# Reordering copies ahead of an attention: written with gaps instead of read with gaps, second value weight split among them, in a fixed order

## The chip, the cores and the metric

The kernel runs on one core of one Trainium2 chip. The core has five engines with a queue of instructions each: TensorE (PE) multiplies matrices, with a weight load (PEld) ahead of each product, VectorE (DVE), ScalarE (ACT) and GpSimd (POOL) work on elements, and SyncE (SP) starts most transfers. An engine takes its instructions in the order in which they stand in its queue, and waits at one whose inputs aren't ready. The metric is the time of one execution on the device in microseconds (us); lower is better.

## The reference

Two transformer layers work on 512 tokens of 1024 features in 32-bit floats. Layer 0 has a gated linear recurrence (HGRN2) as its mixer, layer 1 a dilated attention; each has a SwiGLU feed-forward part behind it. What matters here is the hand-over from the feed-forward part of layer 0 to the attention of layer 1:

```python
h = h + (1.0 + g2) * rms_norm(y, norm_g[layer, 3])          # end of layer 0
u = rms_norm(h, norm_g[layer, 0]) * (1.0 + sc1) + sh1       # start of layer 1
proj = (u @ w_in).reshape(B, S, N_GROUPS, 3, ATT_HEADS, ATT_HEAD_DIM)
for gi, (window, dilation) in enumerate(((128, 1), (512, 4), (2048, 16))):
    q = apply_partial_rope(proj[:, :, gi, 0], cos, sin) * scale
    k = apply_partial_rope(proj[:, :, gi, 1], cos, sin)
    v = proj[:, :, gi, 2]
    o_g, lse_g = dilated_group_attention(q, k, v, window, dilation)
```

A group with dilation 4 attends within tokens that are four apart. For it the kernel keeps a second copy of u whose tokens stand in another order: the 128 tokens l = 0..127 with the same remainder r (token 4l + r) side by side, r after r.

## The kernel before, in words

Every product of two 32-bit numbers is made of three: each operand is split into a high part (the number cast to the type float32r, "hi", "uh") and a low part (what the cast left over, "lo", "ul"), and TensorE adds high x high, high x low and low x high (the helper `three`, L597 to L601). The cast is made by ScalarE, the subtraction by VectorE or GpSimd.

u is kept transposed, as `uh` and `ul`: eight tiles (kt = 0..7) of 128 features by 512 tokens. A weight tile of 512 input features by 512 output features (128 partitions x 2048 numbers, four kt) arrives in a `raw` buffer and is split into `hi` and `lo`; there are two raw buffers and three places for split pairs. The class `Stream` hands them out in the order of a list. `Stream.process_to` (L113, L114) splits a weight in one piece of 2048; `Stream.pieces` (L133, L134) gives the functions that split it in two halves of 1024, so that the caller says where each stands. `Stream.fill` starts the next load as soon as a raw buffer is free; SyncE issues it and waits for the instruction that frees the buffer.

The stage around the change, in order:

- The end of the feed-forward part (`ffn`, manual schedule). For each of four token tiles t the class `Turn` does: squares of the two halves of y on ScalarE (`sq_y`, L635), their product with a gate on VectorE (`gated`, L644), a reciprocal root on VectorE and GpSimd (`r_y`, L648 and L650), the update of h on VectorE with the squares of the new h on ScalarE (`upds`, L660 and L635), a second root (`r_h`), the normalised tile `xn` on VectorE (L674), its transposition on TensorE (`flip`, L680), scale and shift into `u` (L690 on ScalarE, L692 on VectorE), and the split into `uh` (L695, ScalarE) and `ul` (L699, GpSimd). "Manual schedule" means that the instructions of each engine stand in its queue in the order of the code.
- The value projection of attention group 0 (`v_prod`): for each token tile 24 products (8 kt x 3) into one bank of accumulators, `ps_mm`, and one copy into `V[0]` by ScalarE (L1696). Tiles 0 and 1 fill the time in which the last token tiles are normalised; tiles 2 and 3 follow. The two weights of this group are `hi_5909` (kt 0 to 3) and `hi_6077` (kt 4 to 7) in the listings below.
- In the same block, a first weight of group 1 (`hi_6304`, kt 0 to 3) is split in two halves, and four transfers on ScalarE's queue put h aside (`h_away`).
- The copies in the other token order: for each kt one on ScalarE (from `uh` into `apart[0]`, L1721) and one on VectorE (from `ul` into `apart[1]`, L1722). They read every fourth token, so with gaps of 16 bytes, and write 512 numbers in line.
- The value projection of group 1 (`tok_proj`, four tiles of 24 products, evicted at L1704 into `V[1]`), with the second weight of the group (`hi_6402`, kt 4 to 7) split in one piece.
- Sums of the copies over pairs of tiles for a seven-product scheme (`token_sums`, L892 to L896 on VectorE, then cut into new contents of uh and ul, L900 and L901), and then the attention itself, which begins with products of `apart` and the weight `hi_6411`. Its order comes from a planner (`Plan`).

What stands behind the first of these stages, the copies, `tok_proj` and `token_sums`, is not in a manual schedule: there a scheduler that simulates a timeline sets the order in each queue.

Of the kernel before, what the change touches and what calls it, by code (L numbers as in the profile page):

```python
# [11 lines left out]
F32 = mybir.dt.float32  # L12
# [5 lines left out]
P = 128  # L18
S = 512
D = 1024  # L20
KT = D // P
NT = S // P
# [15 lines left out]
SEEN = lambda t: t.rearrange("p (x n a) -> p x a n", a=2, n=P)  # L38
# [277 lines left out]
def block_kernel(tc, x, c, positions, ada_w, ada_b, norm_g, hgrn_w_in, lower, hgrn_norm_g, hgrn_w_out,  # L316
# [8 lines left out]
    with ExitStack() as ctx:  # L325
# [712 lines left out]
        def ffn(l, first, close, nxt, side):  # L1038
            turns.close()
            close()  # L1040
            with ExitStack() as fx:
# [104 lines left out]
                with tc.manual_schedule(engines=ORDERED):  # L1146
# [17 lines left out]
                    for hi_f, lo_f in st.pieces(2, True):  # L1164
                        hi_f()
                        lo_f()
                    st.fill()
                    mm(2, (2, 3))
                    y_steps(2)
                    n.upds(2)  # L1170
                    n.flip(1, [bank("mm"), bank("b")])
# [11 lines left out]
                    vw = [st.take(0), st.take(0)]  # L1183
                    v_prod(vw, 0, range(8))
# [8 lines left out]
                    v_prod(vw, 1, range(8))  # L1193
# [11 lines left out]
                    v_prod(vw, 2, range(8))  # L1205
                    v_prod(vw, 3, range(8))
# [294 lines left out]
        def tok_proj(done):  # L1501

            ws = [st.take(), st.take(1)]
            for t in range(NT):
                ps = bank("mm")
                tok = slice(t * P, (t + 1) * P)
                for kt in range(KT):
                    whi, wlo = ws[kt // 4]
                    w = slice((kt % 4) * 512, (kt % 4 + 1) * 512)
                    three(ps, uh[:, kt, tok], ul[:, kt, tok], whi[:, w], wlo[:, w], kt == 0, kt == KT - 1)  # L1510
                done(t, ps)

# [120 lines left out]
        for p in range(4):  # L1633
            tiles = []
            whi, wlo = st.take()
# [40 lines left out]
        def open_attention():  # L1676
# [8 lines left out]
            banks = {}  # L1685

            def v_prod(ws, t, kts):
                if t not in banks:
                    banks[t] = bank("mm")
                tok = slice(t * P, (t + 1) * P)  # L1690
                for kt in kts:
                    w = slice((kt % 4) * 512, (kt % 4 + 1) * 512)
                    three(banks[t], uh[:, kt, tok], ul[:, kt, tok], ws[kt // 4][0][:, w], ws[kt // 4][1][:, w],
                          kt == 0, kt == KT - 1)
                if kts[-1] == KT - 1:
                    act.copy(PLACED(V[0][:, t]), SEEN(banks[t]))  # L1696
            return v_prod
# [3 lines left out]

        def to_away(t, ps):

            act.copy(PLACED(V[1][:, t]), SEEN(ps))  # L1704
            if t == NT - 1:
                act.dma_start(v_away, V[1])
# [673 lines left out]
```

## Time and profile before

| | |
|---|---|
| median of three runs | 1464.53 us (1464.22 to 1465.02) |
| the profiled execution | 1461.9 us |
| its span, which the profile covers | 1460.2 us |
| mean granted TensorE clock over the span | 0.998 |
| TensorE busy | 1422.7 us, 97% |
| VectorE, ScalarE, GpSimd busy | 1119.6, 825.6 and 196.8 us |
| moved by DMA | 201.10 MB, mean 138 GB/s |

A row of a timeline gives the start of an instruction in us from the start of the span, its duration in us, the engine, the line in the kernel, the operation, what it writes and reads, its shape, and in brackets how long its engine stood idle before it and what ended that wait. Several like instructions in a row are merged (x8), and the duration is then that of all. Matmuls are pipelined: one starts before the one before has ended, so the time between starts is what one costs. A row of the waits says who waited for whom: in total, how often, and the longest. The granted clock is 1.00 at full speed. A few records of matmuls can be missing.

### The profile page before, as it was taken

Reading aid. Unit: us, or ns where it says so; the run is one execution under the profiler, and the core shown is the slowest. Engines: PE = TensorE matmul, PEld = TensorE weight load, DVE = VectorE, ACT = ScalarE, POOL = GpSimd, SP = SyncE. Lnnn points to the kernel's source line nnn. Section 1 sums busy time; section 2 is a strip of 40 time slices with the busy share of each in tenths; the row PEclk is TensorE's granted clock in tenths of the full one; section 3 lists DMA queues with packets and bytes.
Section 4 is the critical chain, followed back from the end, with each engine's and each line's share of the span. In section 5 each row is a group of like instructions: output and inputs, shape, how many; then the busy total and the mean of one; then the engine's idle time right before and its main releaser. Section 6 shows DMA issues by size and latency. Waiting matters only on the chain. (4 is left out here: it accounts for less than half of the span.)

```text
span 1460.2 us, 25343 instructions
## 1 busy us (share of the span) xinstructions
PE 1422.7 (97%) x9903; PEld 1307.8 (90%) x9903; DVE 1119.6 (77%) x1800; ACT 825.6 (57%) x1484; POOL 196.8 (13%) x173
## 2 busy tenths in 40 slices
PE   8999999999999999999999999999999999999998
PEld 6777888889999998887989999998998999999887
DVE  4588589488888889778797977888776978887644
ACT  4433442474555553376748878667895645555332
POOL 1012102030111112240000110001012111110100
PEclk9999999999999999999999999999999999999999
DMA  9666554213344368424244443254353244334541
GB/s 310 195 191 200 173 174 145 87 62 93 106 116 116 117 219 295 156 83 148 91 126 132 120 124 95 72 171 131 95 176 114 87 116 115 112 105 157 178 145 58
DMA packets 212872, 201.10 MB, mean 138 GB/s; under 512 B 8920, under 2 KB 170640, under 8 KB 212496
## 3 DMA queue, kind: packets, MB, share of 16 engines
q1 hardware_dynamic: 209776, 192.71, 42.5%
q10 hardware_dynamic: 1952, 6.65, 1.3%
q8 instruction: 78, 1.28, 0.4%
q0 software_dynamic: 1024, 0.12, 0.2%
q14 instruction: 42, 0.34, 0.1%
HBM read 192.30 MB, written 5.30 MB: 135 GB/s over the span
## 5 line engine op out<-in xcount | busy, mean ns | idle before, releaser
L1843 PE MATMUL ps_mm<-apart,hiq 128*128 128x256 f32 (+1 forms) x608 | 137.5, 320 | 3.9 <-ACT xs L1957 3.2
L114 DVE TENSOR_TENSOR lo<-raw,hi 128x2048 fp32r<-128x2048 f32 x41 | 99.6, 2432 | 45.0 <-ACT hi L113 44.9
L113 ACT CAST hi<-raw 128x2048 fp32r<-128x2048 f32 x41 | 78.1, 1906 | 98.4 <-DMA raw<-in_hgrn_w_in_dram 46.7
L599 PE MATMUL ps_mm<-uh,hi 128*128 128x512 f32 (+1 forms) x368 | 130.4, 354 | 0.0
L600 PE MATMUL ps_mm<-ul,hi 128*128 128x512 f32 (+1 forms) x368 | 128.1, 348 | 1.6 <-DVE ul L699 1.6
L601 PE MATMUL ps_mm<-uh,lo 128*128 128x512 f32 (+1 forms) x368 | 128.1, 348 | 0.0
L1843 PEld LDWEIGHTS ps_mm<-apart,hiq 128*128 128x128 f32 x608 | 99.9, 191 | 10.2 <-ACT xs L1957 3.8
L971 DVE TENSOR_TENSOR loq<-raw,hiq 128x1024 fp32r<-128x1024 f32 x72 | 85.0, 1221 | 20.1 <-ACT hiq L967 20.1
L980 PE MATMUL ps_mm<-th,hiq 128*128 128x256 f32 x360 | 99.1, 275 | 0.0
L980 PE MATMUL ps_mm<-tl,hiq 128*128 128x256 f32 x360 | 99.0, 275 | 0.0
L980 PE MATMUL ps_mm<-th,loq 128*128 128x256 f32 x360 | 99.0, 275 | 0.0
L1843 PE MATMUL ps_mm<-apart,loq 128*128 128x256 f32 (+1 forms) x304 | 95.4, 314 | 0.6 <-DVE loq L1979 0.6
L951 POOL TENSOR_TENSOR raw<-raw 128x512 f32<-128x512 f32 x36 | 47.8, 1327 | 320.1 <-DVE spare L947 165.0
L967 ACT CAST hiq<-raw 128x1024 fp32r<-128x1024 f32 x72 | 72.1, 1047 | 21.4 <-DVE raw L955 16.8
L599 PEld LDWEIGHTS ps_mm<-uh,hi 128*128 128x128 f32 x368 | 69.9, 190 | 12.4 <-issue 5.3
L599 PE MATMUL ps_mm<-hi,oh 128*128 128x512 f32 x208 | 79.0, 381 | 0.0
L600 PE MATMUL ps_mm<-lo,oh 128*128 128x512 f32 x208 | 78.9, 380 | 0.0
L600 PEld LDWEIGHTS ps_mm<-ul,hi 128*128 128x128 f32 x368 | 69.9, 190 | 9.3 <-DVE ul L699 2.0
L1083 ACT CAST oh<-mid 128x512 fp32r<-128x512 f32 x44 | 37.3, 871 | 70.7 <-PE ps_b L600 62.1
L601 PEld LDWEIGHTS ps_mm<-uh,lo 128*128 128x128 f32 x368 | 69.9, 190 | 6.8
L1843 PE MATMUL ps_mm<-uh,hiq 128*128 128x256 f32 x256 | 71.2, 278 | 0.2 <-ACT ps_mm L1932 0.2
L1843 PE MATMUL ps_mm<-uh,loq 128*128 128x256 f32 x256 | 70.5, 275 | 0.0
(478 smaller groups left out, 4774.8 us busy)
## 6 DMA issues: line engine op xcount, KB each, us to landing
raw<-in_ada_w_dram SPq DMA_DIRECT2D x40, 1024.0 KB, 5.8
raw<-in_ffn_w_in_dram SPq DMA_DIRECT2D x144, 256.0 KB, 4.0
raw<-in_ffn_w_out_dram SPq DMA_DIRECT2D x22, 1024.0 KB, 5.7
raw<-in_attn_w_in_dram SPq DMA_DIRECT2D x64, 256.0 KB, 4.3
raw<-in_hgrn_w_in_dram SPq DMA_DIRECT2D x12, 1024.0 KB, 5.5
raw<-in_attn_w_in_dram SPq DMA_DIRECT2D x12, 1024.0 KB, 5.1
raw<-in_ffn_w_in_dram SPq DMA_DIRECT2D x8, 1024.0 KB, 5.1
raw<-in_attn_w_in_dram SPq DMA_DIRECT2D x16, 512.0 KB, 5.2
```

Of the source, the lines that this page charges most:

```text
L113: self.nc.scalar.copy(hi, t)
L114: self.nc.vector.tensor_sub(lo, t, hi.bitcast(F32))
L599: pe.matmul(ps, ah, bh, start=start, stop=False, skip_group_check=part)
L600: pe.matmul(ps, ah, bl, start=False, stop=False, skip_group_check=part)
L601: pe.matmul(ps, al, bh, start=False, stop=stop, skip_group_check=part)
L951: pool.tensor_add(r[:, 2], r[:, 2], r[:, 0])
L967: act.copy(hi, src)
L971: dve.tensor_sub(lo, src, hi.bitcast(F32))
L980: pe.matmul(LAID(ps), w[x][:, a], TAKE(us[kt][y]), start=begin and kt + m == 0, stop=kt == 3 and m == 2, skip_group_check=True)
L1083: act.copy(PLACED(oh), SEEN(mid(f)))
L1843: pe.matmul(LAID(dst()), x, TAKE(y), start=begin and i == 0, stop=i == len(todo) - 1, skip_group_check=True)
```

## The change

Three things are edited. In the last part of the feed-forward block, the second half of the low split of `hi_6077` and the start of the next load (`st.fill`) move from ahead of token tile 2's end to behind its update of h. The copies into the other token order read 512 tokens in line and write with gaps: the pattern `p l r` of the destination goes to remainder 0, 1, 2, 3 in turn, 128 numbers (512 bytes) apart, and then to the next l. And the copies, the last two tiles of group 0's values, all of group 1's values and the splits of two weights, now in halves, come into one manual schedule: three copies, tile 2, two copies, half of tile 3, the split of group 1's second weight, the other half, three copies, the first tile of group 1, the split of the attention's first weight, the other tiles. `tok_proj` is gone; `v_prod` serves both groups. The diff:

```diff
--- before.py
+++ after.py
@@ -1161,13 +1161,15 @@
                     n.xn(1)
                     n.parts_of(0, 1)
                     mm(3, (0, 1))
-                    for hi_f, lo_f in st.pieces(2, True):
-                        hi_f()
-                        lo_f()
-                    st.fill()
+                    (hi_a, lo_a), (hi_b, lo_b) = st.pieces(2, True)
+                    hi_a()
+                    lo_a()
+                    hi_b()
                     mm(2, (2, 3))
                     y_steps(2)
                     n.upds(2)
+                    lo_b()
+                    st.fill()
                     n.flip(1, [bank("mm"), bank("b")])
                     n.u_of(1, 0)
                     n.u_of(1, 1)
@@ -1180,8 +1182,7 @@
                     st.beside(None)
                     fx.close()
                     v_prod = nxt[1]()
-                    vw = [st.take(0), st.take(0)]
-                    v_prod(vw, 0, range(8))
+                    v_prod(0, range(8))
                     n.upds(3)
                     n.flip(2, [bank("mm"), bank("a")])
                     n.r_h(3)
@@ -1190,7 +1191,7 @@
                     n.parts_of(2, 0)
                     n.parts_of(2, 1)
                     n.xn(3)
-                    v_prod(vw, 1, range(8))
+                    v_prod(1, range(8))
                     n.flip(3, [bank("mm"), bank("b")])
                     n.u_of(3, 0)
                     n.u_of(3, 1)
@@ -1202,8 +1203,6 @@
                     st.fill()
                     for t in range(NT):
                         act.dma_start(h_away[t], h[:, t])
-                    v_prod(vw, 2, range(8))
-                    v_prod(vw, 3, range(8))
                 turns.close()
 
 
@@ -1498,18 +1497,6 @@
         head = sc.tile([P, S], F32, name="head")
         pool.memset(head, 0.0)
 
-        def tok_proj(done):
-
-            ws = [st.take(), st.take(1)]
-            for t in range(NT):
-                ps = bank("mm")
-                tok = slice(t * P, (t + 1) * P)
-                for kt in range(KT):
-                    whi, wlo = ws[kt // 4]
-                    w = slice((kt % 4) * 512, (kt % 4 + 1) * 512)
-                    three(ps, uh[:, kt, tok], ul[:, kt, tok], whi[:, w], wlo[:, w], kt == 0, kt == KT - 1)
-                done(t, ps)
-
         C16 = lambda a: a.rearrange("p (c t) -> p c t", t=32)
         B44 = lambda a: a.rearrange("p (b c t) -> p b c t", b=4, c=4)
 
@@ -1682,28 +1669,24 @@
             hx.enter_context(cx)
             vp = cx.enter_context(tc.tile_pool(name="a_v", bufs=1))
             V.extend(vp.tile([P, NT, 512], F32, name=f"V{g}") for g in range(3))
-            banks = {}
-
-            def v_prod(ws, t, kts):
-                if t not in banks:
-                    banks[t] = bank("mm")
-                tok = slice(t * P, (t + 1) * P)
-                for kt in kts:
-                    w = slice((kt % 4) * 512, (kt % 4 + 1) * 512)
-                    three(banks[t], uh[:, kt, tok], ul[:, kt, tok], ws[kt // 4][0][:, w], ws[kt // 4][1][:, w],
-                          kt == 0, kt == KT - 1)
-                if kts[-1] == KT - 1:
-                    act.copy(PLACED(V[0][:, t]), SEEN(banks[t]))
-            return v_prod
+            v_tiles.extend(st.take(0) for _ in range(2))
+            return lambda t, kts: v_prod(0, t, kts)
+
+        v_tiles, v_banks = [], {}
+
+        def v_prod(g, t, kts):
+            if (g, t) not in v_banks:
+                v_banks[g, t] = bank("mm")
+            b, tok = v_banks[g, t], slice(t * P, (t + 1) * P)
+            for kt in kts:
+                whi, wlo = v_tiles[2 * g + kt // 4]
+                w = slice((kt % 4) * 512, (kt % 4 + 1) * 512)
+                three(b, uh[:, kt, tok], ul[:, kt, tok], whi[:, w], wlo[:, w], kt == 0, kt == KT - 1)
+            if kts[-1] == KT - 1:
+                act.copy(PLACED(V[g][:, t]), SEEN(b))
 
         ffn(0, first, h0.close, ((1, 0), open_attention), "right")
         v_away = dpool.tile([P, NT, 512], F32, name="v_away")
-
-        def to_away(t, ps):
-
-            act.copy(PLACED(V[1][:, t]), SEEN(ps))
-            if t == NT - 1:
-                act.dma_start(v_away, V[1])
 
         PNs, PR_h = [h[:, k].rearrange("p (t n) -> p t n", t=4) for k in range(2)], h[:, 2].rearrange("p (t n) -> p t n", t=4)
         flip_no = [0, 0]
@@ -1717,10 +1700,31 @@
         up = upx.enter_context(tc.tile_pool(name="a_u", bufs=1))
         up.tile([P, 64], F32, name="pad")
         apart = [up.tile([P, KT, S], F32R, name=f"apart{k}") for k in range(2)]
-        for kt in range(KT):
-            act.copy(V4(apart[0][:, kt]), L4(uh[:, kt]).bitcast(F32))
-            dve.tensor_copy(V4(apart[1][:, kt]), L4(ul[:, kt]).bitcast(F32))
-        tok_proj(to_away)
+        def apart_of(*kts):
+            for kt in kts:
+                for k, (eng, u) in enumerate(((act.copy, uh), (dve.tensor_copy, ul))):
+                    eng(R4(apart[k][:, kt]), u[:, kt].rearrange("p (l r) -> p l r", r=4).bitcast(F32))
+
+        def split_next():
+            for hi_f, lo_f in st.pieces(2, True):
+                hi_f()
+                lo_f()
+            st.fill()
+
+        with tc.manual_schedule(engines=ORDERED):
+            apart_of(0, 1, 2)
+            v_prod(0, 2, range(8))
+            apart_of(3, 4)
+            v_prod(0, 3, range(4))
+            split_next()
+            v_prod(0, 3, range(4, 8))
+            apart_of(5, 6, 7)
+            v_tiles.extend(st.take(0) for _ in range(2))
+            v_prod(1, 0, range(8))
+            split_next()
+            for t in range(1, NT):
+                v_prod(1, t, range(8))
+            act.dma_start(v_away, V[1])
         th, tl = (t.rearrange("p (a b) n -> p a (b n)", a=4).rearrange("p a (b n) -> p a b n", b=4) for t in (uh, ul))
 
         token_sums(th, tl, h.rearrange("p t (a n) -> p (t a) n", a=2), *apart)()
```

On ScalarE, from the end of the feed-forward block to the first of the new casts of uh (L900), before:

```order
L133 CAST hi_6304<-raw_5913 128x1024 x2
L1204 DMA h_away<-h 128x1024 x4
L1721 CAST apart_6384<-uh 128x512 x8
L1696 COPY V_6188<-ps_mm_6317 128x512
L113 CAST hi_6402<-raw_6083 128x2048
L1696 COPY V_6188<-ps_mm_6343 128x512
L113 CAST hi_6411<-raw_6310 128x2048
L900 CAST uh<-h 128x1024
```

and now:

```order
L133 CAST hi_6304<-raw_5913 128x1024 x2
L1205 DMA h_away<-h 128x1024 x4
L1706 CAST apart_6332<-uh 128x128x4 x3
L1686 COPY V_6188<-ps_mm_6342 128x512
L1706 CAST apart_6332<-uh 128x128x4 x2
L133 CAST hi_6385<-raw_6115 128x1024 x2
L1686 COPY V_6188<-ps_mm_6372 128x512
L1706 CAST apart_6332<-uh 128x128x4 x3
L1686 COPY V_6189<-ps_mm_6415 128x512
L133 CAST hi_6441<-raw_6310 128x1024 x2
```

The eight copies are in three lots; ahead of the split of the second weight of group 1 (`hi_6402` before, `hi_6385` now) stand five of them and one eviction, where there were eight and one. That split is in two halves.

On VectorE, from the split of group 1's first weight (`lo_6305`) on, before:

```order
L134 TENSOR_TENSOR lo_6305<-raw_5913,hi_6304 128x1024 x2
L1722 CAST apart_6385<-ul 128x512 x8
L892 TENSOR_TENSOR h<-apart_6384,apart_6385 128x1024 x4
L893 TENSOR_TENSOR h<-h 128x1024
L114 TENSOR_TENSOR lo_6403<-raw_6083,hi_6402 128x2048
L114 TENSOR_TENSOR lo_6412<-raw_6310,hi_6411 128x2048
L894 TENSOR_TENSOR h<-h 128x1024
L895 SCALAR_TENSOR_TENSOR h<-h 128x1024
L896 SCALAR_TENSOR_TENSOR h<-h 128x1024
```

and now:

```order
L134 TENSOR_TENSOR lo_6305<-raw_5913,hi_6304 128x1024 x2
L1706 CAST apart_6333<-ul 128x128x4 x5
L892 TENSOR_TENSOR h<-apart_6332,apart_6333 128x1024 x2
L134 TENSOR_TENSOR lo_6386<-raw_6115,hi_6385 128x1024
L893 TENSOR_TENSOR h<-h 128x1024
L134 TENSOR_TENSOR lo_6386<-raw_6115,hi_6385 128x1024
L1706 CAST apart_6333<-ul 128x128x4 x3
L892 TENSOR_TENSOR h<-apart_6332,apart_6333 128x1024 x2
L894 TENSOR_TENSOR h<-h 128x1024
L134 TENSOR_TENSOR lo_6442<-raw_6310,hi_6441 128x1024
L895 SCALAR_TENSOR_TENSOR h<-h 128x1024
L134 TENSOR_TENSOR lo_6442<-raw_6310,hi_6441 128x1024
```

Ahead of the first low half of the second weight stand five copies and two of the four sums, where there were eight copies, the four sums and L893. Between its two halves stands L893. The low half of the attention's first weight (`lo_6412`, now `lo_6442`) stands between the last sums.

On VectorE within the feed-forward block, around the end of token tile 2 (`yg_6102` before, `yg_6099` now), before:

```order
L134 TENSOR_TENSOR lo_6078<-raw_5842,hi_6077 128x1024 x2
L644 TENSOR_TENSOR yg_6102<-ps_mm_5189,gate_5393 128x512
L648 TENSOR_SCALAR rv_6104<-ss_6097 128x1
L644 TENSOR_TENSOR yg_6108<-ps_a_5193,gate_5393 128x512
L660 SCALAR_TENSOR_TENSOR h<-yg_6102,rr_6106,h 128x512
L660 SCALAR_TENSOR_TENSOR h<-yg_6108,rr_6106,h 128x512
L692 TENSOR_SCALAR u_6132<-ps_b_6118,cols 128x128 x4
```

and now:

```order
L134 TENSOR_TENSOR lo_6078<-raw_5842,hi_6077 128x1024
L644 TENSOR_TENSOR yg_6099<-ps_mm_5189,gate_5393 128x512
L648 TENSOR_SCALAR rv_6101<-ss_6094 128x1
L644 TENSOR_TENSOR yg_6105<-ps_a_5193,gate_5393 128x512
L660 SCALAR_TENSOR_TENSOR h<-yg_6099,rr_6103,h 128x512
L660 SCALAR_TENSOR_TENSOR h<-yg_6105,rr_6103,h 128x512
L134 TENSOR_TENSOR lo_6078<-raw_5842,hi_6077 128x1024
L692 TENSOR_SCALAR u_6132<-ps_b_6118,cols 128x128 x4
```

One of the two halves of `lo_6078` has moved from ahead of tile 2's gated products, root and update to behind them.

On TensorE the number of products is the same. Before, the scheduler had mixed the four tiles of group 1 with each other and with the end of group 0, so that products with the group's first weight went ahead while the second was still out; now the tiles follow each other one by one, each through kt 0 to 7. The queues of GpSimd and SyncE hold the same instructions in the same order.

## The prediction

> **What bounds the kernel now.** I read the page first, then busy time by stage around the changed place, then the waits there, then the timelines of the engines that the waits name.
>
> ```profile
> span 1460.2 us, 25343 instructions
> ...
> PE 1422.7 (97%) x9903; PEld 1307.8 (90%) x9903; DVE 1119.6 (77%) x1800; ACT 825.6 (57%) x1484; POOL 196.8 (13%) x173
> ```
>
> TensorE is busy 97% of the span. Only its pauses, 37.5 us in all, and time at a lower clock can be won, so the question is which of them lie where the change works. By stage (length, then busy time of TensorE matmul, weight load, VectorE, ScalarE, GpSimd; granted clock; DMA):
>
> ```profile
> 650.00:660.00 10.00, 8.88 (x46) 7.59 (x45) 6.84 (x12) 9.71 (x15) 5.06 (x5) 1.00 0.53 208
> 660.00:670.00 10.00, 7.67 (x36) 6.38 (x34) 9.29 (x12) 10.00 (x9) 0.00 (x0) 1.00 0.39 109
> 670.00:680.00 10.00, 9.00 (x34) 7.61 (x35) 9.93 (x7) 4.29 (x4) 0.00 (x0) 0.83 0.44 125
> ```
>
> Between 650 and 680 us TensorE loses 4.45 us to pauses, and part of the last stretch runs at a lower clock. ScalarE is full from 650 to 670, VectorE from 660 to 680. The waits from 640 to 700 us (total, times, longest):
>
> ```profile
> DVE ul L901 <- ACT uh L900: 5.9, 1, 5.9
> ...
> PE ps_mm L599 <- ACT hi L113: 3.3, 1, 3.3
> ...
> PE ps_mm L680 <- DVE xn L674: 1.1, 1, 1.1
> ```
>
> TensorE waits twice: for the cast of the second half of the second value weight (hi, L113), and for the normalised last token tile that it transposes (xn, L674). Its own timeline shows what they cost:
>
> ```profile
> 651.50 0.63 PE L680 MATMUL ps_mm<-ident,xn 128*128 128x128 f32 x4 [1.12 <-DVE xn L674]
> ...
> 652.32 0.46 PE L599 MATMUL ps_mm<-hi,uh 128*128 128x512 f32 x1
> ...
> 653.05 0.38 PE L599 MATMUL ps_mm<-hi,uh 128*128 128x512 f32 x1
> ...
> 653.70 0.38 PE L599 MATMUL ps_mm<-hi,uh 128*128 128x512 f32 x1
> ...
> 667.29 0.38 PE L599 MATMUL ps_mm<-hi,uh 128*128 128x512 f32 x1
> 671.00 0.48 PE L599 MATMUL ps_mm<-hi,uh 128*128 128x512 f32 x1 [3.33 <-ACT hi L113]
> ...
> 688.55 0.38 PE L601 MATMUL ps_mm<-hi,ul 128*128 128x512 f32 x1
> ```
>
> Three products of one weight tile start 0.65 us apart, 0.216 us each. From 652.32 the kernel has two token tiles of the first value group and four of the second, 24 products each, so the last of the 144 would start at 652.32 + 143 x 0.216 = 683.2. It starts at 688.55: 5.4 us lost, 3.5 of them the pause (667.29 to 671.00 less one product), the rest the lower clock behind it. Why the cast is late, on ScalarE:
>
> ```profile
> 655.75 1.04 ACT L133 CAST hi<-raw 128x1024 fp32r<-128x1024 f32 x1
> 657.01 11.66 ACT L1721 CAST apart<-uh 128x512 fp32r<-128x512 f32 x8 [0.22 <-POOL ul L699]
> 668.57 0.57 ACT L1696 COPY V<-ps_mm 128x512 f32<-128x512 f32 x1
> 669.05 1.90 ACT L113 CAST hi<-raw 128x2048 fp32r<-128x2048 f32 x1
> ```
>
> All eight reordering copies, 1.46 us each (11.66/8), stand ahead of the cast. On VectorE:
>
> ```profile
> 655.88 3.31 DVE L134 TENSOR_TENSOR lo<-raw,hi 128x1024 fp32r<-128x1024 f32 x2 [1.91 <-ACT hi L133]
> 659.11 6.62 DVE L1722 CAST apart<-ul 128x512 fp32r<-128x512 f32 x8
> 665.56 2.43 DVE L892 TENSOR_TENSOR h<-apart,apart 128x1024 f32<-128x1024 f32 x2
> 668.70 2.36 DVE L892 TENSOR_TENSOR h<-apart,apart 128x1024 f32<-128x1024 f32 x2 [0.70 <-ACT apart L1721]
> 670.98 1.22 DVE L893 TENSOR_TENSOR h<-h 128x1024 f32<-128x1024 f32 x1
> 672.11 4.49 DVE L114 TENSOR_TENSOR lo<-raw,hi 128x2048 fp32r<-128x2048 f32 x2
> ```
>
> A copy takes 0.83 us there (6.62/8), a sum or a half split 1.2, and the low half of the late weight comes at 672.1 only.
>
> **Part 1: the low half split behind the update of token tile 2.** The chain to the 1.12 us pause, one or two rows of each engine:
>
> ```profile
> 634.61 3.43 DVE L134 TENSOR_TENSOR lo<-raw,hi 128x1024 fp32r<-128x1024 f32 x2 [1.18 <-ACT hi L133]
> ...
> 640.34 0.63 ACT L635 ACTIVATE junk<-h 128x512 bf16<-128x512 f32 x1 [3.65 <-DVE h L660]
> ...
> 643.87 2.52 POOL L699 TENSOR_TENSOR ul<-u,uh 128x512 fp32r<-128x512 f32 x2 [0.76 <-ACT uh L695]
> 646.34 0.55 POOL L650 TENSOR_TENSOR rr<-rv,expo 128x1 f32<-128x1 f32 x1
> ...
> 650.61 0.74 DVE L674 TENSOR_SCALAR xn<-h,rr 128x1024 f32<-128x1024 f32 x1
> ```
>
> Two halves take 3.43 us and hold up the update of h, for which ScalarE waits 3.65 us; ScalarE's squares, then its uh, then GpSimd's L699, rr and xn follow in order. Taking one half (1.7 us) out brings the update 1.7 us forward. GpSimd must finish its earlier rr first, which eats some 0.4, so xn comes about 1.3 earlier. That covers the pause of 1.12: **gain 1.1 us**, since TensorE can't start before its previous product ends. Bounds: 0, if the half costs as much in its new place (it now stands ahead of VectorE's u of tile 1), and 1.1. The half is needed by the first value product's seventh weight tile, near 643; it ends near 641, so 2 us cover it. The load that follows it, on SyncE's queue, is needed at 663 and goes out about 641, at 5 us a load.
>
> **Part 2: the copies' new form.** They read in line and write four places in turn, 512 bytes apart. The nearest rows are a ScalarE copy that writes with gaps of 16 bytes (L2224), the old copies, and an in-line cast of that size (L695); ns minimum/median/maximum:
>
> ```profile
> L1721 ACT CAST apart<-uh x8: 1097/1603/1701, 657.0 to 667.6; 128x512 fp32r<-128x512 f32 x8
> ...
> L1722 DVE CAST apart<-ul x8: 867/928/958, 659.1 to 664.8; 128x512 fp32r<-128x512 f32 x8
> ...
> L2224 ACT COPY oT<-ps_b x6: 1339/1532/1557, 806.1 to 1038.9; 128x512 f32<-128x512 f32 x6
> ...
> L695 ACT CAST uh<-u x24: 607/618/627, 302.2 to 1138.5; 128x512 fp32r<-128x512 f32 x24
> ```
>
> On ScalarE writing with gaps costs what reading with gaps costs: 1.53 against 1.60. So I take the old prices for both engines, 1.46 and 0.83 from start to start. Ends: 0.6 (L695) to 1.7 (the dearest L1721) on ScalarE; on VectorE, which shows no write with gaps, 0.6 (the in-line price of ScalarE) to 1.56 (ScalarE's dearest L2224). No row has steps of 512 bytes. [...]
>
> **Part 3: the fixed order.** Times are those of before, 1.1 earlier. ScalarE: copies from 655.9; three copies 660.3, first value eviction (0.5) 660.8, two copies 663.7, high halves of the late weight 664.7 and 665.7. VectorE: its earlier split ends at 658.1 (655.88+3.31-1.1), five copies 662.2, two sums 664.6, first low half 665.9 (it also needs the high half of 664.7), one sum 667.1, second low half 668.3. TensorE starts at 651.2; after 60 products (two tiles of 24 and half of the next) it wants the late weight's high half at 664.2, its first low half at 664.4, its second, six products on, at 665.7. So it waits until 668.3: **2.6 us late in two or three pauses**, none over about 1.3 us. With b for a VectorE copy, the last half comes at 658.1 + 5b + 6.0 (two sums, half, sum, half), a delay of 5b-1.6. With a for a ScalarE copy, the high half comes at 655.9 + 5a + 1.5 and the last low half 3.6 later, a delay of 5a-4.7. The larger counts; at 0.83 and 1.46 both give 2.6.
>
> Of the old loss of 5.4, then, 2.8 is won. The other three copies and all evictions stand where nobody waits: VectorE ends its sums near 679, when TensorE's value products still run until about 685. Of the loads, the next weights' (behind the late weight's low half) goes out at 668 and the one after that near 678:
>
> ```profile
> 674.43 2.02 SPq L76 DMA_DIRECT2D raw<-in_attn_w_in_dram  x4
> 676.63 22.66 SPq L85 DMA_DIRECT2D raw<-in_attn_w_in_dram  x2
> ...
> 701.10 1.38 ACT L2023 CAST hiq<-raw 128x1024 fp32r<-128x1024 f32 x1
> ```
>
> The first is 6 us earlier than before, the second 1 us later, and it is used at 701 less the gain: nothing.
>
> **Sum.** 1.1 + 5.4 - 2.6 = 3.9 us. The profiled execution took 1461.9 us (span 1460.2), so it would take 1458.0; the median of the runs is 2.6 above it, at 1464.53, and I carry the difference over: **1460.6 us**. A measurement of this kernel can tell about 0.2%, 2.9 us, from no change.
>
> **Rivals.**
> - *Cheap writes (0.17).* With writes in line in price (a and b 0.6) the delay is 1.4 and the gain 5.1: 1459.4. If VectorE took half that again, the delay goes to nothing and the gain is 6.5: 1458.0. Against it stands L2224.
> - *The clock falls all the same (0.08).* Rows that bear on it, by stage as above:
>
> ```profile
> 672.00:676.00 4.00, 4.00 (x12) 3.23 (x11) 4.00 (x3) 1.23 (x1) 0.00 (x0) 0.57 0.11 30
> ...
> 1000.00:1010.00 10.00, 7.88 (x54) 7.18 (x53) 8.77 (x21) 5.86 (x10) 3.73 (x2) 1.00 0.39 106
> ```
>
>   A pause of 3.5 us was followed by a clock of 0.57, one of 2.1 (busy 7.88 of 10) left it at 1.00. Pauses that add up to 2.6 within 4 us, with seven products between, lie in between. It would cost the old 1.9: gain 2.0, 1462.5. [...]
> - *The attention hands it back (0.12).* VectorE is dense there; a new wait of 1 to 3 us would leave 1462 to 1464. Against it: VectorE's work of the attention begins with the wait of 5.9 us shown among the waits (L901 for L900), and L900 overwrites uh, so it waits for TensorE's last value products. The whole stage moves with TensorE.
> - *Dear writes, slower (0.08).* VectorE's five copies now stand ahead of the low half that TensorE waits for. From b = 1.6 (1.2 if the clock falls too) the delay 5b-1.6 eats the 6.5 us that there are to win. At b = 2.0: 8.4 late, 1.9 for the clock, gain -3.8, 1468.3. For it: no row shows such steps on VectorE, and the steps are long. Against: its old copies cost only 0.83, less than ScalarE's.
>
> The forecast itself has 0.55, its own range 1459.8 to 1461.6 (bounds of part 1 and a tenth of a microsecond per copy). Up to 0.05 of it may be measured as no change. The range of 8 in 10 goes from 1458.0, the cheap end, to 1464.2, nearly all handed back; it leaves out the slower case and the last of the handing back. Faster by over 0.2% (under 1461.6): 0.50 + 0.17 = 0.67. Slower by over 0.2% (over 1467.5): 0.05 of the 0.08. The rest, 0.28, is within.
>
> **What would show it.** The 1.12 us wait for xn is gone; the copies cost 1.3 to 1.7 us on ScalarE and 0.8 to 1.0 on VectorE; TensorE waits 2 to 3 us in all, in its second value group's first tile, for lo of L134 on VectorE, and the clock stays at 1.00 between 660 and 690; the attention's first product comes about 3.9 us earlier, and its waits later on are the old ones. I am wrong if a copy costs under 1.0 or over 2.0 us on ScalarE, if it costs over 1.2 on VectorE, or if the attention's stages take longer than before.

## The result and the profile after

The changed kernel took 1460.01 us (median of 8 runs, 1455.86 to 1462.11), the kernel before 1464.78 beside it (8 runs, 1462.60 to 1468.62): ratio 0.996, with an interval of 0.9944 to 0.9975. It is faster by 4.8 us, where 3.9 was forecast. The profiled execution took 1458.26 us.

Its page, the lines that answer to those shown of before:

```profile
span 1456.5 us, 25346 instructions
...
PE 1423.5 (98%) x9903; PEld 1309.1 (90%) x9903; DVE 1118.5 (77%) x1802; ACT 821.6 (56%) x1486; POOL 196.9 (14%) x173
```

TensorE does the same 9903 products; only its pauses, and its time at the lower clock, can have gone. By stage of 10 us (columns as before):

```profile
650.00:660.00 10.00, 9.18 (x47) 7.86 (x46) 6.20 (x12) 9.71 (x19) 5.58 (x5) 1.00 0.38 150
660.00:670.00 10.00, 9.33 (x44) 7.79 (x43) 10.00 (x14) 9.18 (x11) 0.00 (x0) 1.00 0.53 167
670.00:680.00 10.00, 10.00 (x48) 8.77 (x47) 8.68 (x9) 3.06 (x4) 0.00 (x0) 1.00 0.49 127
```

In the last stretch TensorE is never idle and the clock is 1.00, where it was 0.83. The waits of TensorE from 640 to 700 us:

```profile
PE ps_mm L680 <- DVE xn L674: 1.5, 2, 0.8
PE ps_mm L600 <- DVE lo L134: 0.7, 1, 0.7
```

The wait of 3.3 us for the cast of the late weight (the second weight of group 1) is gone, and 0.7 is left for its second low half. But the wait for xn, which was to go, has become two, 1.5 us in all. To see what each stage gave I use three marks on TensorE: the first transposition of token tile 0's normalised rows (L680), that of the last tile, and the attention's first product. Before and after:

```profile
629.46 0.60 PE L680 MATMUL ps_mm<-ident,xn 128*128 128x128 f32 x4
...
688.76 0.59 PE L1843 MATMUL ps_mm<-apart,hi 128*128 128x512 f32 x2
```

```profile
630.36 0.60 PE L680 MATMUL ps_mm<-ident,xn 128*128 128x128 f32 x4
...
645.86 0.63 PE L680 MATMUL ps_mm<-ident,xn 128*128 128x128 f32 x4 [0.64 <-DVE xn L674]
...
652.93 0.63 PE L680 MATMUL ps_mm<-ident,xn 128*128 128x128 f32 x4 [0.82 <-DVE xn L674]
...
668.08 0.38 PE L599 MATMUL ps_mm<-hi,uh 128*128 128x512 f32 x1
...
669.13 0.48 PE L600 MATMUL ps_mm<-lo,uh 128*128 128x512 f32 x1 [0.67 <-DVE lo L134]
...
685.86 0.59 PE L1847 MATMUL ps_mm<-apart,hi 128*128 128x512 f32 x2
```

From the first mark to the second (the **hand-off**) it took 22.04 us before (651.50 - 629.46) and 22.57 now: 0.53 lost. From there to the attention's first product (the **value stage**) it took 37.26 and takes 32.93: 4.33 won. Together that is 3.80 us, in the place that the prediction named and near its size, but out of terms of which one has the wrong sign. The stretch ahead of the first mark took 0.9 more, that behind the last 0.8 less. The change edits the code of neither, and the executions below vary there by 6 and 4.6 us, so the stages tell the kernels apart better than totals do.

On ScalarE, the copies and the late weight's cast now:

```profile
658.45 3.00 ACT L1706 CAST apart<-uh 128x512 fp32r<-128x512 f32 x3 [0.21 <-POOL ul L699]
661.26 0.62 ACT L1686 COPY V<-ps_mm 128x512 f32<-128x512 f32 x1
661.78 2.24 ACT L1706 CAST apart<-uh 128x512 fp32r<-128x512 f32 x2
663.60 2.22 ACT L133 CAST hi<-raw 128x1024 fp32r<-128x1024 f32 x2
```

And on VectorE:

```profile
660.55 2.99 DVE L1706 CAST apart<-ul 128x512 fp32r<-128x512 f32 x5
663.13 2.56 DVE L892 TENSOR_TENSOR h<-apart,apart 128x1024 f32<-128x1024 f32 x2
665.41 1.42 DVE L134 TENSOR_TENSOR lo<-raw,hi 128x1024 fp32r<-128x1024 f32 x1
666.54 1.41 DVE L893 TENSOR_TENSOR h<-h 128x1024 f32<-128x1024 f32 x1
667.68 1.40 DVE L134 TENSOR_TENSOR lo<-raw,hi 128x1024 fp32r<-128x1024 f32 x1
```

From the start of one to the start of the next, a copy takes 0.52 us on VectorE ((663.13 - 660.55)/5) and 0.94 on ScalarE ((661.26 - 658.45)/3). Before it was 0.81 and 1.45, by the same count in the prediction's rows ((665.56 - 659.11)/8 and (668.57 - 657.01)/8). The second low half ends at 669.08, and TensorE, whose last product ahead of it started at 668.08, goes on at 669.13.

### The profile page after: what moved, and what is told of

It is laid out like the page before. It is cut to its first block, busy times and chain, and to the rows that moved or that the text cites. A ratio compares the mean times of both kernels' runs of the same rounds, so it can differ in the third digit from the quotient of the medians.

```text
span 1456.5 us, 25346 instructions
## 1 busy us (share of the span) xinstructions
PE 1423.5 (98%) x9903; PEld 1309.1 (90%) x9903; DVE 1118.5 (77%) x1802; ACT 821.6 (56%) x1486; POOL 196.9 (14%) x173
## 5 line engine op out<-in xcount | busy, mean ns | idle before, releaser
L113 ACT CAST hi<-raw 128x2048 fp32r<-128x2048 f32 x39 | 74.3, 1906 | 98.5 <-DMA raw<-in_hgrn_w_in_dram 42.5
L114 DVE TENSOR_TENSOR lo<-raw,hi 128x2048 fp32r<-128x2048 f32 x39 | 95.3, 2443 | 44.2 <-ACT hi L113 44.0
```

The lines of the kernel that those rows point to most:

```text
L113: self.nc.scalar.copy(hi, t)
L114: self.nc.vector.tensor_sub(lo, t, hi.bitcast(F32))
```

## The experiments

The theory behind them: the gain lies in the value stage and comes from two things, the late weight's split going ahead of some copies (fixed order) and the copies' cheaper form; the moved low half costs the hand-off 0.5 us, because something of GpSimd now runs beside VectorE's xn. The rivals: that the form is cheap only through the new order, or only on one engine; that the form alone does as much as the order with it; that the hand-off's loss is the new order's doing. Stage times in us, each from its own profiled execution:

| kernel | hand-off | value stage | ahead of the first mark | behind the last |
|---|---|---|---|---|
| before | 22.04 | 37.26 | 629.46 | 771.44 |
| after | 22.57 | 32.93 | 630.36 | 770.64 |
| order with the old form | 22.58 | 34.84 | 634.17 | 772.81 |
| form in the old order | 22.04 | 31.99 | 632.93 | 775.24 |
| new form on ScalarE only | 22.59 | 34.05 | 631.91 | 774.15 |
| new form on VectorE only | 22.60 | 34.67 | 633.24 | 771.69 |
| writes in 16-byte steps | 22.58 | 34.39 | 630.89 | 772.44 |
| low half back | 22.03 | 32.91 | 634.57 | 772.19 |
| low half moved, alone | 22.59 | 37.18 | 632.25 | 770.98 |
| subtraction on VectorE | 21.78 | 32.68 | 628.67 | 771.57 |
| sums behind both low halves | 22.02 | 31.99 | 632.15 | 773.44 |
| form and repaired hand-off | 21.78 | 31.98 | 630.49 | 772.35 |
| the same again | 21.77 | 31.98 | 634.30 | 771.55 |
| the change again | 22.59 | 32.86 | 632.77 | 773.78 |

Where a kernel was profiled twice (the change, the best of both) the two stages repeat within 0.1 us. Of the kernels that ran once, the low half back took 1463.42 us in all, the low half moved alone 1464.74, the sums behind both low halves 1461.33 and the 16-byte steps 1462.04; one run tells nothing at this size.

**Order and form apart.** The change with the copies' old form:

```diff
-                    eng(R4(apart[k][:, kt]), u[:, kt].rearrange("p (l r) -> p l r", r=4).bitcast(F32))
+                    eng(V4(apart[k][:, kt]), L4(u[:, kt]).bitcast(F32))
```

> The changed kernel with the copies in their old form (read with gaps, write in line), in the changed order. Theory now: the price belongs to the form, so the copies cost 1.46 us on ScalarE and 0.83 on VectorE from start to start (1.0 and 0.52 in the changed kernel), the low half is 2.6 us late instead of 0.8, the value stage takes 34.7 us instead of 32.9, and the time is 1.8 us above the changed kernel's, 2 us below before. Rival: the copies got cheaper because they stand in lots, away from other copies; then the value stage stays at 32.9 and the prices at 1.0 and 0.5. The prediction took the old prices and so forecast 2.6 us for the changed kernel itself.

And the kernel before with the copies' new form alone, in the old places of the queues:

```diff
-            act.copy(V4(apart[0][:, kt]), L4(uh[:, kt]).bitcast(F32))
-            dve.tensor_copy(V4(apart[1][:, kt]), L4(ul[:, kt]).bitcast(F32))
+            for k, (eng, u) in enumerate(((act.copy, uh), (dve.tensor_copy, ul))):
+                eng(R4(apart[k][:, kt]), u[:, kt].rearrange("p (l r) -> p l r", r=4).bitcast(F32))
```

> The kernel before with only the copies' new form: order of every queue as before. Theory now: at 1.0 us a copy the late cast comes 3.8 us earlier, just when TensorE wants it, and the low part (about 671.5 us) before the 93rd product behind the last transposition needs it (672.4); the value stage is 31.9 to 32.2 us, 1 us shorter than in the changed kernel, the hand-off 22.0; time 5 us below before. So the form alone does it and the fixed order adds nothing. Rival: the order is what wins; then the value stage stays above 34 us and the gain under 3 us.

The eight copies on each engine, from the lines grouped by form (total us, mean ns of one); old form in the new order, then new form in the old order. For comparison, before has 11.66 and 6.62 us in the rows that the prediction shows.

```profile
L1706 ACT CAST apart<-uh 128x512 fp32r<-128x512 f32 x8 | 11.8, 1530 | 0.2 <-POOL ul L699 0.2
...
L1706 DVE CAST apart<-ul 128x512 fp32r<-128x512 f32 x8 | 6.4, 860 | 0.0
```

```profile
L1722 ACT CAST apart<-uh 128x512 fp32r<-128x512 f32 x8 | 8.0, 1268 | 0.2 <-POOL ul L699 0.2
...
L1722 DVE CAST apart<-ul 128x512 fp32r<-128x512 f32 x8 | 4.5, 864 | 0.0
```

The price belongs to the form, whatever the order: 1.47 and 0.80 us of busy time a copy (11.8/8, 6.4/8) against 1.00 and 0.56 (8.0/8, 4.5/8). Like copies overlap: in the old order the new form takes 1.27 and 0.86 us in the mean, and from start to start 0.93 and 0.49. Busy time counts the tail behind each lot as well. The order alone shortens the value stage by 2.4 us, the form alone by 5.3, which is more than both together (4.3). The waits of the form-alone kernel from 640 to 700 us are one line, and it is not in the value stage:

```profile
PE ps_mm L680 <- DVE xn L674: 1.1, 1, 1.1
```

Timed, the order alone took 1462.58 us (ratio 0.9972, 0.9961 to 0.9983), the form alone 1460.65 (0.9966, 0.9955 to 0.9978). The intervals overlap; the stage times tell the two apart. So the fixed order adds nothing to the form: with it, TensorE takes the tiles one by one and meets the second low half 1 us early. In the old order the low half comes later still:

```profile
672.12 2.68 DVE L114 TENSOR_TENSOR lo<-raw,hi 128x2048 fp32r<-128x2048 f32 x1
```

It ends 19.8 us behind the second mark (674.80 - 654.97), where the change has its last half after 16.2 (669.08 - 652.93), and yet TensorE doesn't wait: the scheduler's mixed order has other products to do until then.

**Which engine.** The change with the new form on ScalarE only:

```diff
-                    eng(R4(apart[k][:, kt]), u[:, kt].rearrange("p (l r) -> p l r", r=4).bitcast(F32))
+                    if k == 0:
+                        eng(R4(apart[k][:, kt]), u[:, kt].rearrange("p (l r) -> p l r", r=4).bitcast(F32))
+                    else:
+                        eng(V4(apart[k][:, kt]), L4(u[:, kt]).bitcast(F32))
```

> The changed kernel with the new form on ScalarE only; VectorE's copies read with gaps as before. Theory: each engine's price belongs to its own form, so ScalarE stays at 1.0 us a copy from start to start and VectorE goes to 0.83; the second low half is 5 x 0.83 - 1.6 = 2.5 us late at most, value stage 34.5 (32.9 in the changed kernel). Rival: it is VectorE's gapped reads that slow ScalarE (alone 1.1, beside them 1.6 in the kernel before); then ScalarE stays at 1.4 to 1.5 whatever its own form.

And on VectorE only, the same with `if k == 1:`.

> The changed kernel with the new form on VectorE only; ScalarE's copies read with gaps as before. Theory: ScalarE 1.46 us a copy, VectorE 0.52; the high half comes 5 x 0.46 = 2.3 us later than in the changed kernel and sets the delay, 5 x 1.46 - 4.7 = 2.6; value stage 34.7. Rival: without gapped reads on VectorE, ScalarE's old form costs 1.0 to 1.1 as well, and the value stage is 33.0.

The copies of the two, ScalarE's and VectorE's of the first, then of the second:

```profile
L1707 ACT CAST apart<-uh 128x512 fp32r<-128x512 f32 x8 | 8.1, 1143 | 0.2 <-POOL ul L699 0.2
...
L1709 DVE CAST apart<-ul 128x512 fp32r<-128x512 f32 x8 | 6.3, 887 | 0.0
```

```profile
L1709 ACT CAST apart<-uh 128x512 fp32r<-128x512 f32 x8 | 11.5, 1503 | 0.2 <-POOL ul L699 0.2
...
L1707 DVE CAST apart<-ul 128x512 fp32r<-128x512 f32 x8 | 4.5, 716 | 0.0
```

Each engine's price follows its own form and not its neighbour's. One engine in the old form is enough to bring back 1.1 us (VectorE) or 1.7 us (ScalarE) of the value stage. One run of each took 1464.39 and 1463.91 us, too few to tell anything.

**Which step.** The change with writes in steps of 16 bytes, as L2224 has them, and reads in line. Its attention gets its rows in another order than it needs, with the same instructions.

```diff
-                    eng(R4(apart[k][:, kt]), u[:, kt].rearrange("p (l r) -> p l r", r=4).bitcast(F32))
+                    eng(L4(apart[k][:, kt]), V4(u[:, kt]).bitcast(F32))
```

> The changed kernel, its copies reading in line as changed but writing one after the other with gaps of 16 bytes, where the change goes round four places 512 bytes apart. So the tokens are not put in the order that the attention needs; the work is of the same size. Theory: the row from which the prediction took its price (a ScalarE copy that writes with 16-byte gaps, 1.53 us) holds for that step and not for the change's, so ScalarE costs 1.4 to 1.5 us from start to start here (1.0 in the changed kernel), VectorE 0.8 (0.52 to 0.6), and the value stage 34.5 to 34.8 us. Rival: any write with gaps is cheap when the copy reads in line from SBUF, and the old row was dear because it reads PSUM; then the prices stay at 1.0 and 0.55 and the stage at 32.9.

```profile
L1706 ACT CAST apart<-uh 128x512 fp32r<-128x512 f32 x8 | 11.5, 1642 | 0.2 <-POOL ul L699 0.2
...
L1706 DVE CAST apart<-ul 128x512 fp32r<-128x512 f32 x8 | 6.1, 1009 | 0.0
```

1.44 and 0.76 us of busy time a copy: writing with gaps of 16 bytes costs nearly what reading with them costs in the same order (1.47 and 0.80), as the row L2224 said. Going round four places 512 bytes apart costs 1.05 and 0.60 by the same count (8.4/8, 4.8/8). So it is mostly the step: of the 1.91 us by which the new form shortens the value stage in this order (34.84 to 32.93), 1.46 come with the step and 0.45 with writing the gaps instead of reading them. Reads in steps of 512 bytes were not tried, and what in the memory makes the long step cheap is not shown by these runs.

**The hand-off.** The change with the low half back in its old place:

```diff
-                    (hi_a, lo_a), (hi_b, lo_b) = st.pieces(2, True)
-                    hi_a()
-                    lo_a()
-                    hi_b()
+                    for hi_f, lo_f in st.pieces(2, True):
+                        hi_f()
+                        lo_f()
+                    st.fill()
                     mm(2, (2, 3))
                     y_steps(2)
                     n.upds(2)
-                    lo_b()
-                    st.fill()
```

> The changed kernel with the end of the feed-forward part as it was before (both low halves ahead of token tile 2's update); copies, splits and order as changed. Measured on TensorE from the first token tile's transposition to the last one's (the hand-off: 22.04 us before, 22.58 in the changed kernel) and from there to the attention's first product (the value stage: 37.26 and 32.93). Theory now: the moved low half cost time, since GpSimd's subtraction of tile 1 then starts 0.9 us earlier and runs beside VectorE's xn; so the hand-off returns to 22.0 with one wait of 1.1 us, xn of tile 2 to 0.75 us, and the value stage stays at 32.9: 0.5 us less than the changed kernel. The prediction's step says that undoing it costs 1.1 us. A third reading, that the fixed order behind it lengthened the hand-off, says that it stays at 22.6.

And the kernel before with this one move (the same lines the other way round):

> The kernel before with only the low half moved behind token tile 2's update. Theory now: hand-off 22.6 us (22.04 before), two waits for xn of 0.6 to 0.8 us, xn of tile 2 at 1.7 us beside GpSimd's subtraction; the value stage as before, 37.3; 0.5 us slower than before, too little for the time to tell. The prediction's step: hand-off 20.9, no wait for xn, 1.1 us faster.

Undone, the hand-off is 22.03 us as before; alone, it is 22.59 as after. The loss belongs to the move and to nothing else of the change. Its way, first on ScalarE after: tile 2's update comes 1.14 us earlier than before (the wait there was 3.65, see the prediction's rows), not 1.7.

```profile
640.10 0.63 ACT L635 ACTIVATE junk<-h 128x512 bf16<-128x512 f32 x1 [2.51 <-DVE h L660]
```

Then VectorE after:

```profile
635.51 2.29 DVE L134 TENSOR_TENSOR lo<-raw,hi 128x1024 fp32r<-128x1024 f32 x1 [1.17 <-ACT hi L133]
...
640.58 1.31 DVE L134 TENSOR_TENSOR lo<-raw,hi 128x1024 fp32r<-128x1024 f32 x1
...
644.02 1.70 DVE L674 TENSOR_SCALAR xn<-h,rr 128x1024 f32<-128x1024 f32 x1
645.64 1.35 DVE L1741 TENSOR_TENSOR maskR<-maskR,V 128x128 f32<-128x128 f32 x1
646.92 0.68 DVE L644 TENSOR_TENSOR yg<-ps_mm,gate 128x512 f32<-128x512 f32 x1
```

GpSimd after:

```profile
634.09 2.64 POOL L699 TENSOR_TENSOR ul<-u,uh 128x512 fp32r<-128x512 f32 x2 [0.53 <-ACT uh L695]
...
643.38 0.61 POOL L650 TENSOR_TENSOR rr<-rv,expo 128x1 f32<-128x1 f32 x1 [1.09 <-DVE rv L648]
643.90 2.95 POOL L699 TENSOR_TENSOR ul<-u,uh 128x512 fp32r<-128x512 f32 x2
```

And VectorE before, the same three instructions (the mask stood ahead of xn there):

```profile
642.98 0.29 DVE L1737 TENSOR_TENSOR maskR<-maskR,V 128x128 f32<-128x128 f32 x1
643.19 0.74 DVE L674 TENSOR_SCALAR xn<-h,rr 128x1024 f32<-128x1024 f32 x1
...
644.94 0.69 DVE L644 TENSOR_TENSOR yg<-ps_mm,gate 128x512 f32<-128x512 f32 x1 [1.00 <-ACT junk L635]
```

The two low halves were never 1.7 us each. The one that stayed takes 2.29, and its start runs beside GpSimd's subtraction of tile 0 (634.09 to 636.73), which may be the same collision as the one below; that leaves 1.14 of the 3.43 for the one that moved. In its new place it stands ahead of u of tile 1 and costs 1.31, so xn of tile 2 starts no earlier: 13.73 us behind the first mark before, 13.66 after. But ScalarE's squares and uh do come earlier, and GpSimd, which before waited 0.76 us for uh and began its subtraction (L699) at 643.87 as xn ended (643.19 + 0.74), now goes on to it straight from rr, as xn starts. xn takes 1.70 instead of 0.74, the mask 1.35 instead of 0.29, the subtraction itself 2.95 instead of 2.52. VectorE's next instruction (yg of the last tile) starts 16.56 us behind the first mark instead of 15.48, and the last xn is 0.53 late. TensorE pays it in two waits, 0.64 and 0.82, where it had one of 1.12. That is 0.34 more; the one pause of the prediction's rows cost it some 0.2 beyond the wait itself (3.49 for 3.33), and now there is one pause more.

In time the three lie together: xn starts 0.12 us after the first of the two L699 (644.02 and 643.90), and the mask starts at 645.64, while they still run, to 646.85. What makes them slow each other is not shown by these runs.

If GpSimd's subtraction beside xn and the mask is the cause, the change needs only the subtraction of tile 1 off GpSimd: on VectorE itself, behind xn.

```diff
-                    n.parts_of(1, 0)
-                    n.parts_of(1, 1)
+                    n.hi_of(1, 0)
+                    n.hi_of(1, 1)
                     n.xn(2)
+                    n.lo_of(1, 0, dve)
+                    n.lo_of(1, 1, dve)
```

> The changed kernel with token tile 1's low part subtracted by VectorE, behind xn of tile 2, where GpSimd did it. Theory (GpSimd's subtraction beside xn slows both): xn of tile 2 takes 0.75 us instead of 1.70, the transposition of tile 2 waits for nothing, GpSimd's root of tile 3 no longer stands behind the subtraction, and the hand-off takes 21.7 us (22.57 in the changed kernel, 22.04 before); value stage 32.9. Rival: xn is slow for another reason (its own wait, the mask work); then it stays at 1.7 and the hand-off at 22.5 or, with 1.4 us more on VectorE, above.

```profile
642.35 0.75 DVE L674 TENSOR_SCALAR xn<-h,rr 128x1024 f32<-128x1024 f32 x1
643.02 0.68 DVE L699 TENSOR_TENSOR ul<-u,uh 128x512 fp32r<-128x512 f32 x1
643.62 0.28 DVE L1743 TENSOR_TENSOR maskR<-maskR,V 128x128 f32<-128x128 f32 x1
```

xn is back at 0.75 us and the mask at 0.28, the subtraction costs VectorE 0.68 a piece where GpSimd needs 1.3, and the hand-off is 21.78: 0.79 less than after, 0.26 less than before. So the collision is shown by its removal. One wait for xn of 0.85 us is left. One run took 1456.45 us.

**The last wait of the value stage.** The change with the low half back as above, and with the sums behind both low halves of the late weight: they now stand inside the block of fixed order, behind group 1's first tile, and the cuts of their results (L900, L901) follow the block.

```diff
+            cut = token_sums(th, tl, h.rearrange("p t (a n) -> p (t a) n", a=2), *apart)
...
-        token_sums(th, tl, h.rearrange("p t (a n) -> p (t a) n", a=2), *apart)()
+        cut()
```

> The changed kernel with the feed-forward part's end as before and, on VectorE, the sums of the copies behind both low halves of the second weight (they stood ahead of the first half and between the two). Theory: the last wait of the fixed order, 0.83 us for the second low half, goes; value stage 32.0 (32.9 in the changed kernel), hand-off 22.0. Rival: the next thing is late at once, the sums or the attention's first weight, and the stage stays near 32.9 or the attention's first products wait.

The value stage is 31.99 us, without a wait; so the sums ahead of and between the two low halves make up the whole wait for the second one. It takes another order to reach what the form reaches in the old one.

**The best of both.** The new form in the old order, with the low half moved and tile 1's subtraction on VectorE:

> The kernel before with the copies' new form, the low half moved as in the change, and tile 1's low part on VectorE behind xn of tile 2; no fixed order for the copies and the value projection. Theory: hand-off 21.7 and value stage 32.0, so 53.7 us from the first transposition to the attention's first product, where before takes 59.3 and the changed kernel 55.5: 5.6 us below before and 1.8 below the changed kernel. Rival: the hand-off's gain is eaten by VectorE, which has 1.4 us more to do, and the sum is that of the form alone, 54.0.

> The new form with the repaired hand-off and without the fixed order, beside the changed kernel on the same chip: stages 21.8 and 32.0, 1.7 us below the changed kernel and 5.5 below before. Rival: the 1.7 us don't show in the time, since the attention waits elsewhere; then the two medians agree within 0.5 us.

With the change itself once more beside the second of them:

> The changed kernel once more, on the chip on which the form with the repaired hand-off is timed. The stages of the first profile should come back: hand-off 22.6, value stage 32.9; time about 3.7 us below before (start-up differs from run to run by several us, so the median over five rounds).

Hand-off and value stage take 53.76 and 53.75 us in the two executions, 55.5 in the change's two and 59.3 before. Timed, it took 1456.93 us (ratio 0.9945, 0.9932 to 0.9958) and 1457.92 (0.9965, 0.9953 to 0.9978); the change again took 1459.15 (0.9966, 0.9954 to 0.9978). The time can't tell the two kernels apart; the 1.7 us between them are shown by the stages alone. Nor do the timings check the stages closely. For two kernels the gain in the two stages lies below the interval of the time: 1.9 us against 2.5 to 5.7 for the order with the old form, and 5.5 against 6.1 to 10.0 for the first timing of the best of both. Where the rest came from is not shown.

## Why the prediction came out, step by step

- **What bounds the kernel** and where: right. The value stage is 31.98 us at best, so before lost 5.28 there; the prediction had 5.4.
- **Part 1, gain 1.1 us: wrong in sign.** Measured -0.53. The step that failed is "xn comes about 1.3 earlier". The mean of two unlike halves (3.43/2) was taken for the price of each; the half was then set down again ahead of u, which the prediction named as its lower bound of 0; and below 0 it named no bound, because it followed the chain of the wait through GpSimd without asking what GpSimd's earlier subtraction would run beside. The halves' 2.29 and 1.14 stood in the trace of before as well, hidden in a row of two.
- **Part 2, old prices for the new form: the size was off.** 1.05 and 0.60 us (8.4/8 and 4.8/8, the page's group below) in place of 1.46 and 0.83, by the prediction's own count. The nearest row, L2224, writes in steps of 16 bytes; at those steps its price nearly holds (1.44), at 512 it doesn't. Both lie within the ends that were named, VectorE's at the lower one; from start to start VectorE's 0.52 is under that end of 0.6.

```profile
L1706 ACT CAST apart<-uh 128x512 fp32r<-128x512 f32 x8 | 8.4, 1258 | 0.2 <-POOL ul L699 0.2
...
L1706 DVE CAST apart<-ul 128x512 fp32r<-128x512 f32 x8 | 4.8, 859 | 0.0
```

- **Part 3, the order: the formulas hold.** A delay of 5b-1.6 or 5a-4.7, the larger of the two, against the value stage less 31.98. Here a and b go from start to start of the five copies that stand ahead of the late weight's split, as each run's rows have them:

| kernel | a, b | by the formulas | measured |
|---|---|---|---|
| after | 0.93, 0.52 | 1.0 | 0.95 |
| old form | 1.50, 0.81 | 2.8 | 2.86 |
| new on ScalarE only | 0.94, 0.76 | 2.2 | 2.07 |
| new on VectorE only | 1.47, 0.51 | 2.65 | 2.69 |
| 16-byte steps | 1.34, 0.67 | 2.0 | 2.41 |

  All but the last, which is 0.4 off, agree within 0.2 us. With the old prices the forecast was 2.6 us late, and the order with the old form is 2.86 late. The clock stayed at 1.00, as expected, so its rival falls.
- **The sum** came near by luck, because two errors lay against each other: 1.6 us too much in part 1, 1.5 too little in the value stage (2.8 forecast, 4.33 measured). What happened is the rival of cheap writes with part 1 taken off: its 5.1 less 1.6 is 3.5, and 3.80 was measured. The gain of 4.8 between the medians holds another 1.0, which neither stage explains; 3.80 lies just within its interval (0.9975 is 3.7 us). The forecast's own range was not quite what its bounds give either: part 1 at 0 alone makes 1461.7, and a tenth of a microsecond less on each of the five copies 1460.1, not 1459.8.
- **The attention hands it back:** not seen. The stretch behind the last mark took 770.64 us against 771.44, but 773.78 in the change's second execution, so this stretch alone can't settle 1 to 3 us. The medians, 4.8 us apart, show no loss against the 3.80 of the stages. **Dear writes** needed b of 1.6; it is 0.5 to 0.6.
- Of what would show it wrong: the copy on ScalarE came in under the limit of 1.0 us from start to start (0.93; 1.05 by busy time), and the wait for xn did not go. TensorE waited 0.67 us for the second low half, not 2 to 3.

## What to carry to other kernels

Before a step is moved up, look at what the engines behind it will start earlier and beside what that will run: here a subtraction on GpSimd that came 0.9 us sooner more than doubled two instructions of VectorE (0.74 to 1.70 us and 0.29 to 1.35). Don't take the price of one instruction from a mean over two, nor that of one step between addresses from another step. And try each part of a change alone: here the cheaper form by itself gave more in its stage than form and new order together.

## What the runs showed that was not expected

**The clock fell behind pauses of 1.9 us.** In the execution of the form-alone kernel the stretch behind the last mark took 775.24 us. In two places there the granted clock stood at 0.50, for 3.4 us each (the mean from 820 to 825 us is 0.66, which is 0.50 for 3.4 of the 5):

```profile
821.60:824.90 3.30, 3.30 (x16) 3.21 (x16) 2.63 (x5) 2.89 (x8) 0.74 (x1) 0.50 0.01 1
1009.30:1012.60 3.30, 3.30 (x18) 3.30 (x18) 2.84 (x13) 3.00 (x6) 0.00 (x0) 0.50 0.00 0
```

Just ahead of each stands one pause of TensorE of less than 2 us:

```profile
821.34 0.62 PE L1843 MATMUL ps_mm<-apart,hiq 128*128 128x256 f32 x2 [1.89 <-ACT xs L1957]
...
1008.69 1.55 PE L2145 MATMUL ps_a<-qk,qk 128*128 128x128 f32 x8 [1.88 <-ACT h L2208]
```

In the second execution of the best of both, the second of these waits was as long, and the clock behind it stayed at 1.00 (the pause, then the stretch):

```profile
1007.65 1.16 PE L2149 MATMUL ps_a<-qk,qk 128*128 128x128 f32 x8 [1.92 <-ACT h L2212]
```

```profile
1008.00:1012.00 4.00, 4.00 (x39) 4.00 (x38) 3.44 (x16) 3.90 (x10) 0.00 (x0) 1.00 0.02 6
```

So the length of the single pause does not decide alone; what does was not tried. Elsewhere the clock fell just behind this second wait of 2.46 us (the change again), and it stayed at 1.00 at waits of 1.82 (the change), 2.12 (before) and 2.3 us (the order with the old form). By these rows a fall is half the clock for 3.4 us, which I estimate at up to 1.7 us (3.4 x 0.5); the falls are one part of why the stretch behind the last mark varies from 770.6 to 775.2 us between executions.

**Copies of the new form overlap on ScalarE.** In the change their mean duration is 1.26 us, but within a lot one starts every 0.93 us, while one in line of that size (L695) takes 0.62. For a run of such copies the time from start to start is the price, not the mean.
